# Modulation of a hybrid diffusion backbone: conditioning rows by DMA, sums of squares on VectorE, other pacing of the modulation sums

## The chip, the cores and the metric

The kernel runs on 1 core of one Trainium2 chip. Its engines are TensorE (PE in the profile; PEld is its loading of weights), VectorE (DVE), ScalarE (ACT), GpSimd (POOL) and SyncE (SP), which here only issues transfers. The metric is the device time of one execution in microseconds, the median of several.

## The reference

The reference is a backbone of two layers over 512 latent tokens and 256 context tokens, 1024 channels wide, batch 1, all in float32. Cut to what matters here:

```python
for l in range(2):
    mod_l = split(silu(c) @ w_mod[l] + b_mod[l], 6)        # latent: shift, scale, gate, twice
    mod_c = split(silu(c_ctx) @ w_mod[l] + b_mod[l], 6)    # context
    h  = rms_norm(x, norm1_g[l]) * (1 + mod_l[1]) + mod_l[0]
    hc = rms_norm(xc, norm1_g[l]) * (1 + mod_c[1]) + mod_c[0]
    # one input projection of h and hc, three mixers (neighbourhood attention, gated
    # recurrence, windowed attention), a branch projection each, merged by sigmoid gates: m
    x = x + mod_l[2] * (m @ w_out[l])
    h2 = rms_norm(x, norm2_g[l]) * (1 + mod_l[4]) + mod_l[3]
    x = x + mod_l[5] * (square(relu(h2 @ w_ff1[l])) @ w_ff2[l])
    # in layer 0 the context xc goes through the same with mod_c; layer 1 only reads it
return rms_norm(x, final_g)
```

In layer 1 the context needs only its first shift and scale, since it is not updated there. The modulation has 48 chunks of 128 output channels in each layer (8 chunks for each of the 6 parts).

## The kernel before

Channels lie on the 128 partitions and tokens on the free axis: a tensor of 1024 channels is 8 tiles of 512 latent and 256 context columns. Each float32 product is made of three passes over rounded high and low parts (`PASSES`, L310), so each weight tile is loaded by SP (L248), rounded by ScalarE (L258) and subtracted on DVE (L259), four tiles ahead of its use.

The program is written in one order by hand, and that order is each instruction's priority; a planner then sets each engine's own order, and an instruction can be put ahead of its place in the program when what it needs is there. Each engine then runs its list in order. All large tiles of SBUF come from one pool of 50 slots (`t3`).

Work beside the main chain of products is written as generators. `pump` (L183) is called after each group of matmuls with the time that they should take; each side queue (`attn`, `lru`, `misc`) takes one step of its generator whenever a `period` of such time has come together. `finish_but(side, n)` steps a queue at once until n generators are left.

`sil_rows` (L387) makes the silu of both conditioning vectors as rows on all partitions: 16 broadcast products with the identity on PE (L394), evacuated by ScalarE (L395). `mod_chunks` (L402) is the modulation: w_mod lies transposed in memory, so for each chunk of output channels and each half of the 1024 inputs a tile of 128 x 512 is loaded (L411), and for each of latent and context one instruction of DVE (L420) multiplies it with the row and sums along the free axis. After 16 tiles the sums of 8 chunks are closed (L430 to L437): `gt1` is the gate of the first residual, `G1` and `G2` are the scales of the two norms. Chunks 0 to 15 of layer 0 are made otherwise, at the start. In layer 0, chunks 16 to 23 (the first gate), 24 to 39 (shift and scale of the second norm) and 40 to 47 (the last gate) are put into `misc` when the gates and the last branch begin (L1196 to L1200), with two tiles loaded ahead; all of layer 1 follows during the MLP of layer 0 (L1297 to L1300), with six.

The output projection (L1233 to L1255) makes column tiles 0 to 3 for both segments, then 4 to 7 for the latent columns, then 4 to 7 for the context. `x_add` (L1231) adds each to the residual stream, and `Sumsq.add` (L474, L479) squares the result on ScalarE and adds the squares up: the first 6 of 7 adds on POOL, the last on DVE. `rstd` sums over partitions by PE (L484), takes the power -0.5 on POOL (L487) with one Newton step on DVE, and spreads the result by PE (L495). `n2` makes the normed and modulated tiles (`normed`, L508 to L510). The MLP starts with `gemm_first` (L337). After layer 1, `n1` writes the output of the final norm (L1331, L1334), in two halves of 256 columns.

Of the kernel before, what the change touches and what calls it, by code (L numbers as in the profile page):

```python
# [9 lines left out]
AF = mybir.ActivationFunctionType  # L10
ALU = mybir.AluOpType
# [3 lines left out]
D = 1024  # L15
# [3 lines left out]
L = 2  # L19
P = 128  # L20
# [5 lines left out]
NFF = 8  # L26
WA = 4
LB = 3.436
PM1 = 1.954
MA = 2  # L30
PS = 0.75
RK = 1
POOLSS = 8
NF = 1
NG = 1
BA = ((1, 1, 1, 1), (2, 2, 0, 0))
# [10 lines left out]
WH = 12  # L47
PA = 1.789
PL = 1.398
PM = 1.106  # L50
HPS = {'gate10': 60, 'ws': -50, 'relu': 60, 'gate01': 60, 'xp': 60, 'gx': 20, 'sink1': 400}
GO = [(x[0], int(x[1]), int(x[2])) for x in GO]
EPS = 1e-6
# [65 lines left out]
def build(tc, A, out):  # L119
    nc = tc.nc  # L120

    with ExitStack() as es:
# [11 lines left out]
        def t3(name, dt=F32):  # L134
            cnt[0] += 1
            return big.tile([P, W], dt, tag="t3", name=f"{name}_{cnt[0]}")
# [24 lines left out]
        def ps_s():  # L161
            cnt[0] += 1
            return pss.tile([P, 512], F32, tag="S", name=f"S_{cnt[0]}")
# [124 lines left out]
        class Seg:  # L288
            def __init__(self, s, cols, ps):
                self.s, self.cols, self.ps = s, cols, ps  # L290
                self.n = cols.stop - cols.start
# [77 lines left out]
        mk = [const.tile([P, 2, 2], F32, name=f"mk{k}") for k in range(8)]  # L369
        xsp = drp.tile([8, P, T], F32, name="xsp")  # L370

        nc.scalar.dma_start(cc, A["cc"])
        nc.sync.dma_start(kc[:, 0:K_PERM], A["kc"][:, 0:K_PERM])
        for l in range(L):
            nc.scalar.dma_start(sm[l], A["sm"][l])
# [10 lines left out]

        def sil_rows():  # L387

            for n in range(4):
                silB.append(t3("sil"))  # L390
                ps = ps_s()
                for k in range(4):
                    c = 2 * (4 * (n % 2) + k) + n // 2
                    mm(ps[:, k * P:(k + 1) * P], sil[:, c:c + 1].to_broadcast([P, P]), ident, start=True, stop=True)  # L394
                act(silB[n][:, 0:512], ps, AF.Copy)  # L395
            silB.append(t3("junk"))

        def finish_but(side, n):
            while len(side.q) > n:
# [2 lines left out]
        def mod_chunks(l, lo, hi, ahead):  # L402

            seq = [(c, i) for c in range(lo, hi) for i in range(2)]
            raws = deque()

            def ld(n):
                if n < len(seq):
                    c, i = seq[n]
                    r = t3("mr")  # L410
                    nc.sync.dma_start(r[:, 0:512], A["w_mod"][l, c][:, i * 512:(i + 1) * 512])  # L411
                    raws.append(r)

            for n in range(ahead):
                ld(n)
            yield
            for n, (c, i) in enumerate(seq):
                r = raws.popleft()
                for s in range(2):
                    V.scalar_tensor_tensor(  # L420
                        r[:, 0:512] if s else silB[4][:, 0:512], r[:, 0:512], 1.0, silB[2 * s + i][:, 0:512], op0=ALU.mult, op1=ALU.mult, accum_out=mpart[:, i, s, c:c + 1]
                    )
                    yield
                r = None
                ld(n + ahead)
                if n % 16 == 15:
                    g = c // 8
                    cs = slice(8 * g, 8 * g + 8)
                    for s in range(2):
                        V.tensor_tensor(modT[l][:, s, cs], mpart[:, 0, s, cs], mpart[:, 1, s, cs], op=ALU.add)  # L430
                        V.tensor_tensor(modT[l][:, s, cs], modT[l][:, s, cs], sm[l][:, O_BM + 8 * g:O_BM + 8 * g + 8], op=ALU.add)
                        if g == 1:
                            V.scalar_tensor_tensor(G1[l][:, s], modT[l][:, s, cs], 1.0, sm[l][:, O_N1:O_N1 + 8], op0=ALU.add, op1=ALU.mult)
                        if g == 2:
                            V.tensor_scalar(gt1[l][:, s], modT[l][:, s, cs], 0.5, None, op0=ALU.mult)
                        if g == 4:
                            V.scalar_tensor_tensor(G2[l][:, s], modT[l][:, s, cs], 1.0, sm[l][:, O_N2:O_N2 + 8], op0=ALU.add, op1=ALU.mult)  # L437
# [23 lines left out]


        class Sumsq:
            def __init__(self, pool=POOLSS):
                self.pool = pool
                self.acc = {}
                self.n = {}

            def add(self, x, seg):
                s = t3("sq")  # L470
                c = seg.cols
                a = self.acc.get(seg)
                with hp("ss"):
                    act(s[:, c], x[:, c], AF.Square)  # L474
                    if a is None:
                        self.acc[seg] = s
                    else:
                        self.n[seg] = self.n.get(seg, 1) + 1
                        (nc.gpsimd if self.n[seg] < self.pool else V).tensor_tensor(a[:, c], a[:, c], s[:, c], op=ALU.add)  # L479

        def rstd_sum(acc, seg, ps):
            nt = seg.n // P
# [170 lines left out]
            x.append(t)  # L653
        x0 = x
        hs0 = hs = []
        ss0 = ss = Sumsq(0)
        for k in range(8):
            ss.add(x[k], SL)
        rbl = t3("rb")
# [85 lines left out]
        for l in range(L):  # L745
# [448 lines left out]
                    gate(("wi", l, 34 + j), gb[-1])  # L1194
            finish(lru)
            if l == 0:  # L1196
                sil_rows()
                misc.period = PM
                for lo, hi in ((16, 24), (24, 40), (40, 48)):
                    misc.add(mod_chunks(0, lo, hi, MA))  # L1200
            mhl = []
# [13 lines left out]
                branch(yb, 1, jp, sink2)  # L1215
            yb = h = m = None
            finish_but(misc, 2)


            wide[0] = 1 if WIDE & 2 else 0  # L1220
# [56 lines left out]
            for fb in range(NFF + 1):  # L1277
                if fb < NFF:
                    lst = [pair("a") for _ in range(4)]
                    af[fb] = lst  # L1280
                    if fb == 0:
                        rs_ = [t3("r") for _ in range(4)]

                        def mlp_done(i, seg, ps):
                            with hp("relu"):
                                relu2(rs_[i], ps, seg)
                            if seg is HS[0] and i < 3:
                                return
                            for n in range(4) if seg is HS[0] else (i,):
                                relu2_end(rs_[n], lst[n], seg.cols)  # L1290

                        got = [w_get("w1", l, i) for i in range(4)]
                        w_ahead()
                        gemm_first(got.__getitem__, h2, HS, mlp_done, range(4), [(range(4), range(8))])
                        got = None
                        rs_ = None
                        if l + 1 < L:  # L1297
                            finish(misc)
                            misc.period = PM1
                            misc.add(mod_chunks(l + 1, 0, 48, 6))  # L1300
                    else:
                        for i in range(4):
                            w = w_get("w1", l, 4 * fb + i)
                            w_ahead()
                            r = t3("r")
                            for seg in FS:
                                relu2(r, gemm1(w, 0, h2, seg), seg)
                            relu2_end(r, lst[i], CA)
                if fb > 0:
                    if fb == NFF:  # L1310
                        wide[0] = 1 if WIDE & 8 else 0
                    a = af.pop(fb - 1)
# [6 lines left out]
                    if fb == NFF:  # L1319
                        order = [(jp, seg, (0, 1)) for seg in HS for jp in range(4)]  # L1320
                        hs = []

                        def n1(seg, k, rb, x=x, hs=hs, l=l):
                            if l + 1 < L:
                                normed(hs, k, x[k], rb, G1[l + 1][:, seg.s, k:k + 1], modT[l + 1][:, seg.s, k:k + 1], seg, seg.s == 0)
                                return
                            if k % 2 == 0:
                                fin.append(t3("out"))
                            o = fin[-1]
                            i = k % 2  # L1330
                            V.scalar_tensor_tensor(o[:, i * 256:(i + 1) * 256], x[k][:, seg.cols], sm[0][:, O_FG + k:O_FG + k + 1], rb, op0=ALU.mult, op1=ALU.mult)  # L1331
                            if i:
                                q0 = seg.cols.start - PAD
                                nc.sync.dma_start(out[k - 1:k + 1, :, q0:q0 + 256].rearrange("k p n -> p k n"), o[:, 0:512].rearrange("p (k n) -> p k n", k=2))  # L1334

                        fin = []

                        def second(ss=ss, n1=n1, seg=HS[1]):
                            rb = rstd(ss.acc[seg], seg)
                            for k in range(8):  # L1340
                                n1(seg, k, rb)

                    for jp, seg, jjs in order:
# [22 lines left out]
def layouts(np, i):  # L1366
# [16 lines left out]
    xt = np.concatenate([i["x"][0], i["ctx"][0]], axis=0)  # L1383
    d["xc"] = np.ascontiguousarray(xt.T).reshape(8, P, T)
    cc = np.stack([i["c"][0], i["c_ctx"]], axis=0)
    d["cc"] = np.ascontiguousarray(cc.reshape(2, 8, P).transpose(2, 1, 0)).reshape(P, 16)
    d["w_mod"] = np.ascontiguousarray(i["w_mod"].transpose(0, 2, 1)).reshape(L, 48, P, D)
    d["w_mod0"] = np.ascontiguousarray(i["w_mod"][0, :, 0:2048].reshape(8, P, 2, 8, P).transpose(3, 1, 0, 2, 4)).reshape(8, P, 2048)
    d["w_in"] = cols(i["w_in"], 1024)
# [84 lines left out]
```

## Time and profile before

| | |
|---|---|
| time, median of 3 runs (lowest to highest) | 2294.87 us (2293.21 to 2295.03) |
| the profiled execution's own time | 2291.37 us |
| its span, first to last instruction | 2289.6 us |
| PE busy | 2258.2 us, 99% |
| DVE busy | 1477.4 us, 65% |
| ACT busy | 1016.4 us, 44% |
| POOL busy | 93.6 us, 4% |
| mean granted TensorE clock | 0.994 |

The span is one execution. Matmuls are pipelined, so the length of one overlaps the next: where a busy PE has no gaps, the distance of two starts is what one costs. The granted clock is a share of full speed, 2.4 GHz; the lower level is 1.2 GHz. Idle time of an engine other than the one that sets the pace costs nothing.

### The profile page before, as it was taken

What the parts mean: (1) busy time and instruction counts of PE and PEld (TensorE: products, weight loads), DVE (VectorE), ACT (ScalarE), POOL (GpSimd) and SP (SyncE); (2) the same over time, 40 slices, a digit from 0 to 9 for tenths busy, and PEclk for the clock granted to TensorE, in tenths of its full rate; (3) what the DMA queues carried; (4) which work ended last, traced back from release to release, by engine and by line L of the source; (5) the groups of instructions that cost most, each with busy time, mean ns of one, the idle gap of its engine ahead of it and who ended that gap; (6) DMA issues with size and microseconds to landing.
All of it is one profiled execution on the core that took longest, in us unless ns stands there. A gap on an engine that the chain in (4) does not pass through costs nothing.

```text
span 2289.6 us, 34042 instructions
## 1 busy us (share of the span) xinstructions
PE 2258.2 (99%) x13364; PEld 1918.0 (84%) x13364; DVE 1477.4 (65%) x3149; ACT 1016.4 (44%) x1868; POOL 93.6 (4%) x78
## 2 busy tenths in 40 slices
PE   8999999999999999999999999999999999999998
PEld 6888888888888888888888887888888789888887
DVE  5776545677668998776665468664467776444444
ACT  4666545667622242222222246654575844332331
POOL 0000000000100200000000020000000102000001
PEclk8999999999999999999999999999999999999999
DMA  7101111112135343343332132112112242222221
GB/s 275 65 32 44 47 65 50 34 51 70 65 124 199 133 170 129 134 138 129 103 120 95 65 118 77 56 47 74 52 60 88 88 148 93 101 92 100 93 92 65
DMA packets 79856, 216.58 MB, mean 95 GB/s; under 512 B 9296, under 2 KB 12496, under 8 KB 79696
## 3 DMA queue, kind: packets, MB, share of 16 engines
q1 hardware_dynamic: 79264, 214.27, 27.0%
q8 instruction: 105, 1.72, 0.3%
q14 instruction: 55, 0.45, 0.1%
q10 hardware_dynamic: 432, 0.14, 0.0%
HBM read 208.08 MB, written 5.24 MB: 93 GB/s over the span
## 4 chain that ended last, share of the span: by engine, by line
PE 88%; DVE 7%; ACT 3%; issue 1%; DMA 1%; POOL 0%; ACTq 0%; POOLq 0%; DVEq 0%; SPq 0%
PE gl L310 38%; PE S L310 30%; PE gc L310 5%; PE O L616 4%; PE S L598 3%; PE gl L337 2%; PE S L546 2%; PE S L547 2%; DVE wl L259 1%; PE S L337 1%; DVE mr L420 1%; DVE junk L420 1%; ACT tau L1071 1%; DMA wm<-in_w_mod_dram 1%; ACT wh L258 0%
## 5 line engine op out<-in xcount | busy, mean ns | idle before, releaser
L259 DVE TENSOR_TENSOR wl<-wr,wh 128x1024 fp32r<-128x1024 f32 (+1 forms) x276 | 333.8, 1210 | 281.5 <-PE S L310 101.9
L258 ACT ACTIVATE wh<-wr 128x1024 fp32r<-128x1024 f32 (+1 forms) x276 | 287.9, 1045 | 444.2 <-DMA wr<-in_w_ff_dram 254.3
L310 PE MATMUL gl<-hh,wh 128*128 128x512 f32 (+1 forms) x936 | 353.3, 377 | 4.7 <-DVE KL L789 2.1
L310 PE MATMUL gl<-hh,wl 128*128 128x512 f32 (+1 forms) x936 | 347.9, 372 | 0.0
L310 PE MATMUL gl<-hl,wh 128*128 128x512 f32 (+1 forms) x936 | 347.0, 371 | 0.0
L310 PE MATMUL S<-hh,wl 128*128 128x512 f32 (+1 forms) x704 | 247.8, 352 | 1.0 <-DVE wl L259 1.0
L310 PE MATMUL S<-hh,wh 128*128 128x512 f32 (+1 forms) x704 | 247.8, 352 | 0.2 <-ACT tau L1071 0.2
L310 PE MATMUL S<-hl,wh 128*128 128x512 f32 (+1 forms) x704 | 246.9, 351 | 0.0
L310 PEld LDWEIGHTS gl<-hh,wh 128*128 128x128 f32 x936 | 176.1, 188 | 37.7 <-issue 10.1
L310 PEld LDWEIGHTS gl<-hl,wh 128*128 128x128 f32 x936 | 176.3, 188 | 32.6 <-issue 0.9
L310 PEld LDWEIGHTS gl<-hh,wl 128*128 128x128 f32 x936 | 176.2, 188 | 25.6 <-issue 0.5
L310 PEld LDWEIGHTS S<-hh,wh 128*128 128x128 f32 x704 | 132.3, 188 | 20.4 <-ACT tau L1071 0.4
L310 PEld LDWEIGHTS S<-hh,wl 128*128 128x128 f32 x704 | 132.2, 188 | 20.4 <-DVE wl L259 1.5
L310 PEld LDWEIGHTS S<-hl,wh 128*128 128x128 f32 x704 | 132.4, 188 | 19.9 <-issue 0.3
L574 ACT ACTIVATE P<-S,s 128x512 f32<-128x512 f32 (+1 forms) x160 | 102.9, 646 | 84.6 <-DVE s L570 41.2
L310 PE MATMUL S<-ah,wl 128*128 128x512 f32 (+1 forms) x384 | 137.0, 357 | 0.0
L310 PE MATMUL S<-al,wh 128*128 128x512 f32 (+1 forms) x384 | 136.8, 356 | 0.0
L310 PE MATMUL S<-ah,wh 128*128 128x512 f32 (+1 forms) x384 | 136.6, 356 | 0.0
L420 DVE SCALAR_TENSOR_TENSOR junk<-mr,sil 128x512 f32<-128x512 f32 x160 | 110.6, 691 | 24.2 <-DMA mr<-in_w_mod_dram 24.1
L310 PE MATMUL gl<-ah,wl 128*128 128x512 f32 (+1 forms) x352 | 124.3, 353 | 0.0
L310 PE MATMUL gl<-al,wh 128*128 128x512 f32 (+1 forms) x352 | 124.3, 353 | 0.0
L310 PE MATMUL gl<-ah,wh 128*128 128x512 f32 (+1 forms) x352 | 124.2, 353 | 0.0
(344 smaller groups left out, 4836.7 us busy)
## 6 DMA issues: line engine op xcount, KB each, us to landing
wr<-in_w_ff_dram SPq DMA_DIRECT2D x128, 512.0 KB, 3.5
wr<-in_w_in_dram SPq DMA_DIRECT2D x100, 512.0 KB, 3.5
mr<-in_w_mod_dram SPq DMA_DIRECT2D x160, 256.0 KB, 4.4
wr<-in_w_branch_dram SPq DMA_DIRECT2D x24, 512.0 KB, 3.5
wm<-in_w_mod_dram SPq DMA_DIRECT2D x32, 256.0 KB, 6.0
wr<-in_w_out_dram SPq DMA_DIRECT2D x16, 512.0 KB, 3.6
bias<-in_bias_dram SPq DMA_DIRECT2D x16, 256.0 KB, 4.0
x<-in_xc_dram SPq DMA_DIRECT2D x8, 384.0 KB, 7.1
```

Source lines behind the costliest of these rows:

```text
L258: act(h_, r, AF.Copy)
L259: V.tensor_tensor(l_, r, f(h_), op=ALU.subtract)
L310: mm(o, w[wi_][:, c0 + k * P:c0 + (k + 1) * P], view(acts[k][xi]), start=(k == 0 and i == 0), stop=(k == n - 1 and i == 2))
L337: mm(os_[i], w[wi_][:, k * P:(k + 1) * P], seg.nat(acts[k][xi]), start=(k == 0 and p_ == 0), stop=(k == n - 1 and p_ == 2))
L420: V.scalar_tensor_tensor(r[:, 0:512] if s else silB[4][:, 0:512], r[:, 0:512], 1.0, silB[2 * s + i][:, 0:512], op0=ALU.mult, op1=ALU.mult, ...
L546: mm(d, qs[:, qc:qc + P], rk, start=True, stop=False)
L547: mm(d, qs[:, qc:qc + P], rl, start=False, stop=True)
L574: act(p[:, 0:n0], self.S[i][:, 0:n0], AF.Exp, bias=nm[:, i:i + 1], accum_out=su[:, i:i + 1])
L598: nc.tensor.transpose(d, self.p[i][:, j * P:(j + 1) * P], ident)
L616: mm(o[half, oc:oc + P], vt[:, vc:vc + 64], h["pt"][:, j * P:(j + 1) * P], start=(j == 0), stop=(j == nt - 1), tile_position=(0, 64 * h["h ...
L1071: act(tau[ax][half, seg.cols], z[HALF[ax]], AF.Tanh, scale=0.5, bias=bcol)
```

## The change

The two conditioning vectors come a second time in the input `cc`, along the free axis and repeated on all 128 partitions, and `sil_rows`, now a generator at the head of `misc`, loads them and makes the silu with a Tanh on ScalarE and one instruction on DVE each; its factor 0.5 goes into L420. `Sumsq.add` does all adds on DVE. In layer 1 the sums of the context are left out from chunk 16 on. The pacing has other periods: `PM` 1.25 instead of 1.106, a new one of 2.4 (`PMW`) from the output projection of layer 0 on, and `PM1` 2.35 instead of 1.954; the last chunks of layer 0 are finished one block of the MLP later. In the last half of the output two of eight tiles are made by ScalarE and POOL and written by ScalarE's queue.

```diff
-PM1 = 1.954
+PM1 = 2.35
-POOLSS = 8
-PM = 1.106
+PM = 1.25
+PMW = 2.4
...
-        nc.scalar.dma_start(cc, A["cc"])
+        nc.scalar.dma_start(cc, A["cc"][:, 0:16])
...
         def sil_rows():
 
+            for n in range(5):
+                silB.append(t3("sil"))
+                if n < 4:
+                    nc.sync.dma_start(silB[n][:, 0:512], A["cc"][:, 16 + 512 * n:16 + 512 * (n + 1)])
+            yield
             for n in range(4):
-                silB.append(t3("sil"))
-                ps = ps_s()
-                for k in range(4):
-                    c = 2 * (4 * (n % 2) + k) + n // 2
-                    mm(ps[:, k * P:(k + 1) * P], sil[:, c:c + 1].to_broadcast([P, P]), ident, start=True, stop=True)
-                act(silB[n][:, 0:512], ps, AF.Copy)
-            silB.append(t3("junk"))
+                act(silB[4][:, 0:512], silB[n][:, 0:512], AF.Tanh, scale=0.5)
+                V.scalar_tensor_tensor(silB[n][:, 0:512], silB[4][:, 0:512], 1.0, silB[n][:, 0:512], op0=ALU.add, op1=ALU.mult)
+                yield
...
+            ns = lambda c: 2 if l + 1 < L or c < 16 else 1
...
-                for s in range(2):
+                for s in range(ns(c)):
                     V.scalar_tensor_tensor(
-                        r[:, 0:512] if s else silB[4][:, 0:512], r[:, 0:512], 1.0, silB[2 * s + i][:, 0:512], op0=ALU.mult, op1=ALU.mult, accum_out=mpart[:, i, s, c:c + 1]
+                        r[:, 0:512] if s else silB[4][:, 0:512], r[:, 0:512], 0.5, silB[2 * s + i][:, 0:512], op0=ALU.mult, op1=ALU.mult, accum_out=mpart[:, i, s, c:c + 1]
                     )
...
-                    for s in range(2):
+                    for s in range(ns(c)):
                         V.tensor_tensor(modT[l][:, s, cs], mpart[:, 0, s, cs], mpart[:, 1, s, cs], op=ALU.add)
...
             def add(self, x, seg):
...
-                with hp("ss"):
-                    act(s[:, c], x[:, c], AF.Square)
-                    if a is None:
-                        self.acc[seg] = s
-                    else:
-                        self.n[seg] = self.n.get(seg, 1) + 1
-                        (nc.gpsimd if self.n[seg] < self.pool else V).tensor_tensor(a[:, c], a[:, c], s[:, c], op=ALU.add)
+                act(s[:, c], x[:, c], AF.Square)
+                if a is None:
+                    self.acc[seg] = s
+                else:
+                    V.tensor_tensor(a[:, c], a[:, c], s[:, c], op=ALU.add)
...
             if l == 0:
-                sil_rows()
                 misc.period = PM
+                misc.add(sil_rows())
                 for lo, hi in ((16, 24), (24, 40), (40, 48)):
                     misc.add(mod_chunks(0, lo, hi, MA))
...
             finish_but(misc, 2)
+            misc.period = PMW
...
                         if l + 1 < L:
-                            finish(misc)
                             misc.period = PM1
                             misc.add(mod_chunks(l + 1, 0, 48, 6))
...
                 if fb > 0:
+                    if fb == 1 and l + 1 < L:
+                        finish_but(misc, 1)
...
-                        def second(ss=ss, n1=n1, seg=HS[1]):
+                        def second(ss=ss, n1=n1, seg=HS[1], x=x, l=l):
                             rb = rstd(ss.acc[seg], seg)
-                            for k in range(8):
+                            if l + 1 == L:
+
+                                xg = t3("xg")
+                                for i in range(2):
+                                    act(xg[:, i * 256:(i + 1) * 256], x[6 + i][:, seg.cols], AF.Copy, scale=sm[0][:, O_FG + 6 + i:O_FG + 7 + i])
+                                rbs = t3("rb")
+                                act(rbs[:, 0:256], rb, AF.Copy)
+                                for i in range(2):
+                                    nc.gpsimd.tensor_tensor(xg[:, i * 256:(i + 1) * 256], xg[:, i * 256:(i + 1) * 256], rbs[:, 0:256], op=ALU.mult)
+                                nc.scalar.dma_start(out[6:8, :, 256:512].rearrange("k p n -> p k n"), xg[:, 0:512].rearrange("p (k n) -> p k n", k=2))
+                            for k in range(8 if l + 1 < L else 6):
                                 n1(seg, k, rb)
```

## Rows read from the trace of the kernel before

**Rows 1.** The page: busy us of each engine, share of the span, instructions.
```profile
PE 2258.2 (99%) x13364; PEld 1918.0 (84%) x13364; DVE 1477.4 (65%) x3149; ACT 1016.4 (44%) x1868; POOL 93.6 (4%) x78
```
**Rows 2.** Stretches of 50 us: busy us of each engine, clock, DMA share.
```profile
750.00:800.00 50.00, 46.41 (x257) 40.55 (x256) 45.95 (x114) 10.13 (x15) 11.68 (x9) 0.97 0.31 106
...
850.00:900.00 50.00, 50.00 (x287) 43.60 (x286) 49.66 (x120) 14.67 (x22) 0.00 (x0) 1.00 0.45 153
...
1300.00:1350.00 50.00, 49.12 (x282) 42.41 (x282) 24.52 (x40) 13.11 (x22) 11.36 (x9) 1.00 0.31 106
```
**Rows 3.** What PE waited for, whole span: us in total, times, longest.
```profile
PE S L484 <- DVE sq L479: 5.1, 2, 3.6
```
**Rows 4.** PE's timeline: start, us of one, instruction, idle before it and releaser.
```profile
785.16 0.28 PE L310 MATMUL gl<-mmh,wh 128*128 128x256 f32 x1
...
787.64 0.28 PE L310 MATMUL gl<-mmh,wh 128*128 128x256 f32 x1
791.52 1.35 PE L484 MATMUL S<-ones,sq 128*128 128x1 f32 x8 [3.59 <-DVE sq L479]
...
793.09 0.41 PE L310 MATMUL gl<-mml,wh 128*128 128x256 f32 x1
...
795.60 0.28 PE L310 MATMUL gl<-mml,wh 128*128 128x256 f32 x1
...
803.73 0.40 PE L337 MATMUL gl<-hh,wh 128*128 128x512 f32 x1
```
**Rows 5.** Two stretches of the output projection: PE, PEld, DVE, ACT, POOL, clock.
```profile
743.40:787.30 43.90, 43.90 (x235) 37.51 (x235) 43.57 (x107) 8.97 (x13) 12.92 (x9) 1.00 0.48 168
...
791.50:795.50 4.00, 3.98 (x21) 3.98 (x22) 2.33 (x6) 0.42 (x1) 1.04 (x1) 0.58 0.23 68
```
**Rows 6.** The tile of the conditioning rows: ns least, median, most; first and last start.
```profile
L394 PE MATMUL S<-kc,sil x32: 270/275/275, 658.5 to 661.9; 128*128 128x128 f32 x32
```
**Rows 7.** DVE's timeline in the output projection of layer 0.
```profile
753.81 1.26 DVE L431 TENSOR_TENSOR modT<-modT,sm 128x8 f32<-128x8 f32 x1
...
781.68 0.69 DVE L420 SCALAR_TENSOR_TENSOR mr<-mr,sil 128x512 f32<-128x512 f32 x1
...
787.04 0.28 DVE L437 SCALAR_TENSOR_TENSOR G<-modT,sm 128x8 f32<-128x8 f32 x2
...
789.26 0.74 DVE L1231 SCALAR_TENSOR_TENSOR x<-S,gt,x 128x512 f32<-128x512 f32 x1
...
797.90 0.75 DVE L508 SCALAR_TENSOR_TENSOR nt<-x,G,S 128x512 f32<-128x512 f32 x1 [0.99 <-PE S L495]
799.50 0.75 DVE L510 SCALAR_TENSOR_TENSOR hl<-nt,modT,hh 128x512 fp32r<-128x512 f32 x1 [0.85 <-ACT hh L509]
```
**Rows 8.** POOL's timeline: an add of 512 columns, and one of 256.
```profile
753.41 1.64 POOL L479 TENSOR_TENSOR sq<-sq,sq 128x512 f32<-128x512 f32 x1 [3.99 <-ACT sq L474]
...
2278.24 0.72 POOL L479 TENSOR_TENSOR sq<-sq,sq 128x256 f32<-128x256 f32 x1 [0.69 <-ACT sq L474]
```
**Rows 9.** The tile of the squares, adds on DVE: ns least, median, most.
```profile
L479 DVE TENSOR_TENSOR sq<-sq,sq x22: 417/426/695, 6.0 to 2279.6; 128x256 f32<-128x256 f32 x13, 128x512 f32<-128x512 f32 x9
```
**Rows 10.** Stretches of L420 on DVE alone: busy us (events, two per sum), clock.
```profile
662.20:703.30 41.10, 21.40 (x64) 1.00 0.45 149
...
852.00:902.00 50.00, 27.09 (x81) 1.00 0.46 156
```
**Rows 11.** The chain that ended last: start, us, what.
```profile
687.41 5.57 PE gl L310 x24
```
**Rows 12.** SP's timeline: transfers issued.
```profile
766.70 4.01 SPq L411 DMA_DIRECT2D mr<-in_w_mod_dram  x8
```
**Rows 13.** Timelines of PE and of DVE at the end.
```profile
2282.31 0.71 PE L495 MATMUL S<-kc,r 128*128 128x128 f32 x4 [1.62 <-DVE r L490]
...
2283.06 3.22 DVE L1331 SCALAR_TENSOR_TENSOR out<-x,sm,S 128x256 f32<-128x256 f32 x8 [0.81 <-PE S L495]
```
**Rows 14.** Groups by shape: a copy of 256 columns from PSUM, busy us, mean ns.
```profile
L601 ACT ACTIVATE P<-S 128x256 f32<-128x256 f32 x32 | 11.3, 382 | 8.8 <-PE S L598 8.8
```

More of the change, by code (lines that the diff above doesn't have):

```diff
@@ L463, in build, with __init__ @@
         class Sumsq:
-            def __init__(self, pool=POOLSS):
-                self.pool = pool
+            def __init__(self):
                 self.acc = {}
-                self.n = {}
             def add(self, x, seg):
@@ L655, in build @@
         hs0 = hs = []
-        ss0 = ss = Sumsq(0)
+        ss0 = ss = Sumsq()
         for k in range(8):
@@ L1385, in layouts @@
     cc = np.stack([i["c"][0], i["c_ctx"]], axis=0)
-    d["cc"] = np.ascontiguousarray(cc.reshape(2, 8, P).transpose(2, 1, 0)).reshape(P, 16)
+    d["cc"] = np.concatenate([cc.reshape(2, 8, P).transpose(2, 1, 0).reshape(P, 16), np.broadcast_to(cc.reshape(1, 2 * D), (P, 2 * D))], axis=1)
     d["w_mod"] = np.ascontiguousarray(i["w_mod"].transpose(0, 2, 1)).reshape(L, 48, P, D)
```

## The prediction

> **What bounds the kernel now.** I read the busy shares first. TensorE (PE) is busy for 2258.2 of 2289.6 us [rows 1], so only two things can move the time: matmuls that go away, and PE's 31 us of idle time. The table by 50 us stretches says where that idle time lies. From 850 to 1300 us there is none, even where VectorE (DVE) is busy for 49.66 of 50 us; 3.6 us lie between 750 and 800, 0.9 between 1300 and 1350 [rows 2]. Of the waits of PE the longest is that of L484, the sum of squares over partitions, for the add of L479: 5.1 us in two places [rows 3]. The larger place is in layer 0, in the second half of the output projection: PE stops at 787.8 and goes on at 791.52, and then issues a 256-column matmul every 0.21 us (0.41 shown) until 795.60, where 0.28 is shown and one starts every 0.12 [rows 4]. The table gives the reason: granted clock 0.58 from 791.5 to 795.5, between the two levels of 1.2 and 2.4 GHz, behind an idle PE [rows 5]. So the stop cost 3.6 us of idle time and 4.0 x 0.42 = 1.7 us of clock, 5.3 us in all.
>
> Why was the add late? From 743.4 to 787.3 DVE was busy for 43.57 of 43.9 us, and GpSimd (POOL) ran nine adds of L479, 12.92 us [rows 5]. The DVE timeline has the x_add of the last column tile at 789.26, some 4 us after PE went on to the next tile at 785.16, behind modulation sums of L420 and small operations [rows 4, 7]. DVE lost time to POOL as well: an L431 over eight elements took 1.26 us and ended at 755.07, as the POOL add did that began at 753.41 [rows 7, 8]. Nine DVE instructions of that stretch are lengthened in this way, by 0.42 to 1.1 us, 7.6 us together.
>
> **The conditioning rows.** Removed are 16 broadcast products; the trace has 32 PE instructions for them, 658.4 to 661.9 us, 275 ns each and one every 0.11 us [rows 6]. PE works without a break on both sides, so this is 3.5 us off its path. In their place come four loads of 256 KB on SP, some 0.5 us of issue each by the eight like them [rows 12], ahead of the weight loads of that moment; weights are split four tiles ahead, so 2 us of delay is covered; without that cover it would be up to 2 us. Four Tanh replace four Copies of the same size on ScalarE (the gates around them are Tanh too), and four scalar_tensor_tensor of 0.69 us are new on DVE: 2.8 us, hidden, since PE does not wait there. The load of cc still moves 64 bytes for each partition, now with a stride: nothing, and at most some tenths at the start.
>
> **The pacing.** A step is one generator step, one L420 mostly. The pump counts 5.12 units for 24 matmuls of 512 columns, which take 5.57 us [rows 11]: 1.09 us per unit. From the start of the modulation to the output projection there are 4 gates x 7.68 + 8 branch halves x 3.84 = 61.4 units. Before: 61.4 / 1.106 = 55 steps; the first chunk takes 34 (one to load, 32 sums, one to close), 37.6 units or 41 us, and the trace has its 32 sums between 662.2 and 703.3 [rows 10]: the count holds. 21 steps go into the second chunk, the 64 sums behind shift and G2 of the second norm. After: 49 steps, of which 6 are the conditioning rows and 34 the first chunk, leaving 9. Up to the forced finish in the last third of the output projection there are 4 x 7.68 + 4 x 5.12 + 2.56 = 53.8 units: 48 steps before, which ends the chunk, and 53.8 / 2.4 = 22 after. So 30 sums stand ahead of the forced finish and 34 in a lump behind it, in front of the first n2 on DVE.
>
> Whether that lump hurts depends on whether DVE runs sums ahead of their place in the program. In layer 1's chunks it does: in 852 to 902 us there are 81 events, two per sum, so 40 sums, where the pace of 1.954 units (2.13 us) sets 23 [rows 10]. Loads do too: eight were issued from 766.70 on [rows 12], six tiles beyond the pace. I take it that free DVE time is filled this way. Then DVE's work from 743.4 to G2 decides. G2 was done at 787.3 [rows 7]. Added: by the pace 13 sums of the second chunk are done at 743.4 where 22 were, so 9 more at 0.69 us [rows 7], 6.2 us (bounds: 0 if DVE runs ahead as in layer 1, 9.7 if only 8 are done). Added: nine adds on DVE, six at 0.69 and three at 0.42 [rows 9], 5.4 us. Gone: the 7.6 us that POOL took (bounds 0 and 12.9). That gives 791.3. Needed is G2 at: first w1 matmul at 803.73 less the 5.3 us of the stop, 798.4, less the 2.35 us from the L508 at 797.90 to the end of its L510 [rows 4, 7]: 796.0. So the lump is in time with 5 us to spare, and the x_add, which now stands ahead of it, is taken at once: the 5.3 us of the stop go.
>
> One rule speaks against this. The Trainium skill, "Perfetto Trace Analysis", section "Optimizing Scalar/DVE Operations", advises moving work off a saturated DVE, GpSimd included, though it adds that the two share an SBUF port and this may not help; the change moves adds onto a saturated DVE. By the advice alone G2 would be at 787.3 + 6.2 + 5.4 = 798.9, 2.9 us late, and the total about -3.
>
> By the rows, POOL's adds held DVE for 7.6 us, more than the 5.4 that they cost there; I keep 791.3.
>
> In layer 1 DVE is spared 64 sums, 44 us, between 840 and 1225, where PE never idles [rows 2]: nothing. Moving the last chunk's finish past the next w1 block likewise.
>
> **The other adds.** At the end of layer 0 DVE sets the pace for some 10 us within 1300 to 1350 (PE idle 0.88) [rows 2]; six adds of 0.42 fall in there, less what POOL held: +0.7 (bounds 0 and +2). In the output projection of layer 1 I take nothing (bounds -1 and +1).
>
> **The tail.** The eight L1331 of the last half take 3.22 us from 2283.06, 0.40 each; two go to ScalarE and POOL: -0.8 for DVE. The other way starts at the same rb (2283.02) [rows 13]: a copy from PSUM of 0.38 [rows 14], two multiplies of some 0.72 [rows 8], and its DMA at about 2285.0, before DVE's last at 2285.5. So -0.8 (bounds 0 and -1.2).
>
> **Sum.** -3.5 -5.3 +0.7 -0.8 = -8.9 us. The profiled execution took 2291.37 (span 2289.6), so 2282.5; the median of the runs shown is 2294.87, 3.5 above, so I forecast 2286.0.
>
> **The rivals.** (1) The lump is late, by place: DVE fills little ahead, since tiles or loads are short. Sums stay where the program puts them: 34 x 0.69 = 23.5 us from about 789, G2 at 812.5, first w1 matmul at 814.9 instead of 798.4: 16.5 us idle and some 2 us at the lower clock, so -8.9 + 18.5 = +9.6: 2304. It decides once G2 is later than 796 by more than 9 us. For it: the trace before never ran the second chunk ahead. Against it: sums and loads that ran ahead [rows 10, 12]. (2) G2 slips by a few us, because DVE fills its gaps only partly, or POOL's 7.6 us do not come back (798.9 instead of 791.3): 3 to 6 us idle with the clock behind it, in total about -3: 2292. For it: DVE's 43.57 of 43.9 us; against it: that the lengthened rows end with POOL's adds [rows 5, 7, 8]. The advice cited above would end here. (3) The stop stays, since DVE's order still puts sums before the last x_add: only matmuls and tail go, -3.6: 2291. For it: in 743 to 787 DVE had no gap; against it: POOL's part of that goes.
>
> **How the numbers follow.** Forecast 0.48, rival 1 0.17, rival 2 0.20, rival 3 0.15. The measurement can tell about 0.2% (4.6 us) from no change. Faster by more: 0.45 of the forecast's 0.48 and 0.07 of rivals 2 and 3, 0.52. Slower: rival 1 and a bad end of 2, 0.18. Within: 0.30. The range goes from 2281 (all lower bounds, -12, and the spread of the runs) to 2300, which leaves out the full form of rival 1; the likeliest case by itself has 2281 to 2290.
>
> **What would show it.** Right: no matmul at the line of the broadcast; the wait of L484 in layer 0 under 1 us and clock 1.00 there; no L431 over 1 us; G2 before 796 less 3.5; the last out write 0.8 us sooner against the last matmul. Wrong: PE idle in front of the first w1 matmuls of layer 0, with L508 waiting for the L437 of G2; or PE idle in a new place.

## The result and the profile after

The changed kernel takes 2311.2 us (median of 4 runs, 2310.71 to 2312.92) where the kernel before takes 2294.69: a ratio of 1.0075, interval 1.0057 to 1.0092, 16.5 us slower. The profiled execution took 2310.88 us, with a span of 2309.1. Several line numbers are shifted: the sums of L420 are L423 now, their loads L414, the add of squares L478, the sum over partitions L483, the spread L494, the first instruction of `n2` L507, the last tiles L1332.

I first read the busy shares on the page of the changed kernel, which answer to [rows 1], and the stretches that answer to [rows 2, 5], with the columns of those.

```profile
PE 2256.9 (98%) x13332; PEld 1915.6 (83%) x13332; DVE 1456.4 (63%) x3061; ACT 1019.0 (44%) x1871; POOL 43.6 (2%) x32
```

```profile
750.00:800.00 50.00, 45.15 (x263) 39.19 (x261) 31.84 (x77) 9.11 (x13) 1.04 (x1) 0.99 0.40 133
800.00:850.00 50.00, 30.52 (x151) 25.48 (x152) 44.09 (x116) 15.20 (x27) 0.70 (x1) 0.77 0.25 86
...
743.40:787.30 43.90, 43.90 (x236) 37.35 (x234) 28.74 (x69) 8.62 (x12) 1.04 (x1) 1.00 0.24 81
```

DVE now has room where it had none: 28.74 of 43.9 us before 787.3, against 43.57 [rows 5]. But right behind, PE works for only 30.52 of 50 us. The waits of PE say for what, and its timeline shows where:

```profile
PE gl L337 <- ACT hh L508: 25.0, 2, 23.5
...
PE S L483 <- DVE sq L478: 1.8, 1, 1.8
```

```profile
783.73 1.05 PE L483 MATMUL S<-ones,sq 128*128 128x1 f32 x8
...
788.04 1.16 PE L494 MATMUL S<-kc,r 128*128 128x128 f32 x8 [0.67 <-DVE r L489]
...
819.28 0.80 PE L337 MATMUL gl<-hh,wh 128*128 128x512 f32 x1 [23.46 <-ACT hh L508]
819.87 0.63 PE L337 MATMUL gl<-hh,wl 128*128 128x512 f32 x1
820.30 0.63 PE L337 MATMUL gl<-hl,wh 128*128 128x512 f32 x1
```

The stop of [rows 4] is gone: L483 begins with no wait; the 1.8 us left are those of the tail. In its place PE waits 23.46 us for the first normed tile, and then starts a matmul of 512 columns every 0.43 us where the first experiment below has 0.23. DVE's timeline has the reason: the first half of the second chunk (the sums of chunks 24 to 31, for the shift) closes at 779.57, the other half stands behind the square root (L485), and G2 (L440) behind that.

```profile
779.57 0.29 DVE L434 TENSOR_TENSOR modT<-modT,sm 128x8 f32<-128x8 f32 x2
781.54 0.75 DVE L1231 SCALAR_TENSOR_TENSOR x<-S,gt,x 128x512 f32<-128x512 f32 x1 [1.68 <-PE S L310]
...
784.82 0.16 DVE L485 TENSOR_SCALAR v<-S 128x4 f32<-128x4 f32 x1 [1.14 <-PE S L483]
...
790.02 0.69 DVE L423 SCALAR_TENSOR_TENSOR sil<-mr,sil 128x512 f32<-128x512 f32 x1 [1.20 <-DMA mr<-in_w_mod_dram]
...
816.51 0.69 DVE L423 SCALAR_TENSOR_TENSOR mr<-mr,sil 128x512 f32<-128x512 f32 x1
...
817.53 0.28 DVE L440 SCALAR_TENSOR_TENSOR G<-modT,sm 128x8 f32<-128x8 f32 x2
817.73 0.74 DVE L507 SCALAR_TENSOR_TENSOR nt<-x,G,S 128x512 f32<-128x512 f32 x1
```

The view of stretches for L423 alone (two events per sum) counts them: 22 sums from 730 to 784.8, and 32 from there to G2. The next fence has the stretches of all engines again, where the clock stands beside PE's idle time:

```profile
730.00:784.80 54.80, 14.90 (x44) 1.00 0.38 139
784.90:817.60 32.70, 21.11 (x64) 0.71 0.63 217
```

```profile
799.00:819.00 20.00, 0.00 (x0) 0.00 (x0) 19.13 (x58) 2.60 (x3) 0.00 (x0) 0.50 0.43 159
819.30:823.00 3.70, 3.70 (x10) 2.87 (x11) 2.91 (x5) 1.12 (x3) 0.00 (x0) 0.57 0.00 0
823.00:827.00 4.00, 4.00 (x19) 3.22 (x18) 3.51 (x8) 1.66 (x3) 0.00 (x0) 1.00 0.45 131
```

With PE idle the granted clock is 0.50, the lower level; it is 0.57 for 3.7 us after the start, 1.6 us of work lost. SP's timeline, against [rows 12], shows the loads of those sums:

```profile
759.62 2.33 SPq L414 DMA_DIRECT2D mr<-in_w_mod_dram  x5
785.52 0.33 SPq L248 DMA_DIRECT2D wr<-in_w_ff_dram  x1
785.94 2.76 SPq L414 DMA_DIRECT2D mr<-in_w_mod_dram  x6
792.06 0.33 SPq L248 DMA_DIRECT2D wr<-in_w_ff_dram  x1
792.49 6.60 SPq L414 DMA_DIRECT2D mr<-in_w_mod_dram  x10
```

Before, between the same two weight loads, it had

```profile
766.32 0.33 SPq L248 DMA_DIRECT2D wr<-in_w_ff_dram  x1
766.70 4.01 SPq L411 DMA_DIRECT2D mr<-in_w_mod_dram  x8
793.53 7.52 SPq L248 DMA_DIRECT2D wr<-in_w_ff_dram  x2
```

so eight loads from 766.70 on; now five at 759.62, then none until a weight load that waited 23.5 us for PE to free its tile went out at 785.52.

The account by stretches, from events that both traces have (the matmul that waits for L868/L867 `Q`, DVE's first instruction on `gb`, L1150/L1149, the last matmul of the output projection, the spread at the end of layer 0, the last matmul of w2):

| stretch | before | after | difference |
|---|---|---|---|
| start to `Q` | 90.86 | 90.57 | -0.3 |
| to the first `gb` (conditioning rows) | 574.19 | 570.93 | -3.3 |
| to the end of the output projection | 138.68 | 134.32 | -4.4 |
| PE idle in front of w1 | 0 | 23.46 | +23.5 |
| first w1 matmul to the end of layer 0 | 534.59 | 536.71 | +2.1 |
| layer 1, to the last w2 matmul | 939.93 | 940.75 | +0.8 |
| to the end | 11.35 | 12.36 | +1.0 |

The sum is +19.4, the spans differ by 19.5. The medians differ by 16.5 only: the profiled execution of before was 3.3 us faster than its median here, that of after 0.3. In which stretch those 3 us lie the table can't say.

### The profile page after: what moved, and what is told of

Same layout as the page of the kernel before. It is cut to its first block, busy times and chain, and to the rows that moved or that the text cites. A ratio compares the mean times of both kernels' runs of the same rounds, so it can differ in the third digit from the quotient of the medians.

```text
span 2309.1 us, 33849 instructions
## 1 busy us (share of the span) xinstructions
PE 2256.9 (98%) x13332; PEld 1915.6 (83%) x13332; DVE 1456.4 (63%) x3061; ACT 1019.0 (44%) x1871; POOL 43.6 (2%) x32
## 4 chain that ended last, share of the span: by engine, by line
PE 90%; DVE 5%; ACT 2%; issue 2%; DMA 1%; POOL 0%; SPq 0%; DVEq 0%; POOLq 0%; ACTq 0%
PE gl L310 38%; PE S L310 31%; PE gc L310 5%; PE O L615 4%; PE S L597 3%; PE gl L337 2%; PE S L545 2%; PE S L546 2%; PE S L337 1%; DVE wl L259 1%; DMA wr<-in_w_in_dram 1%; ACT tau L1070 1%; DVE KL L788 0%; DVE mr L423 0%; DVE sil L423 0%
## 5 line engine op out<-in xcount | busy, mean ns | idle before, releaser
L423 DVE SCALAR_TENSOR_TENSOR sil<-mr,sil 128x512 f32<-128x512 f32 x160 | 109.9, 687 | 33.4 <-DMA mr<-in_w_mod_dram 32.7
```

The costliest lines, as they stand in the source:

```text
L423: V.scalar_tensor_tensor(r[:, 0:512] if s else silB[4][:, 0:512], r[:, 0:512], 0.5, silB[2 * s + i][:, 0:512], op0=ALU.mult, op1=ALU.mult, ...
```

## The experiments

The theory (T): the lump of sums behind `finish_but(misc, 1)` costs all of the loss, and the rest of the change gains about what was forecast. The first rival (R1): the adds moved to DVE made it late. Ratios are to the kernel before on the same chip.

**The old pace, all else as changed.**

```diff
-PM = 1.25
-PMW = 2.4
+PM = 1.106
+PMW = 1.106
```

> The kernel after, with both periods of the modulation in layer 0 back at 1.106 (PM and PMW); conditioning rows, adds on VectorE and the new tail stay. Theory T (the lump): the slower pace leaves 32 sums of the second chunk, and their loads, in one lump ahead of the first tile of the second norm, and TensorE waits 23.5 us for it. With the old pace the lump is 2 or 3 sums, G2 is done before 796 us, the first w1 matmul waits under 2 us, and of the forecast's -8.9 us all is left but the tail's error of 1.8: about 2287.6 us (2284 to 2291). Rival R1 (the adds): VectorE is late because it has taken over the nine adds of GpSimd, 5.4 us of work in the stretch before G2; the pace only says where the sums stand. Then G2 stays late, the wait of the first w1 matmul stays over 10 us, and the time is 2300 to 2311.

Measured: 2286.91 us, 0.9970 (0.9959 to 0.9981). Two sums are left behind the square root, G2 starts at 788.86, PE waits for nothing in front of w1. Its first two w1 matmuls:

```profile
794.57 0.39 PE L337 MATMUL gl<-hh,wh 128*128 128x512 f32 x1
794.80 0.40 PE L337 MATMUL gl<-hh,wl 128*128 128x512 f32 x1
```

R1 has fallen: the adds are still on DVE.

**The new pace alone, in the kernel before.**

```diff
-PM = 1.106
+PM = 1.25
+PMW = 2.4
...
             finish_but(misc, 2)
+            misc.period = PMW
```

> The kernel before, with the two periods of layer 0 alone (1.25 for the gates and branches, 2.4 from the output projection on). Everything else is that of before, the broadcast products and the adds on GpSimd too. Theory T: 26 to 30 sums stand in the lump; at 0.73 us each, with two weight subtractions of 1.22 between, from about 790 us on, G2 comes at 811 to 815 instead of 787, and TensorE waits some 10 to 15 us in front of w1, with about 2 us of clock behind it, while the stop of 5.3 us at the sum over partitions goes, since fewer sums stand ahead of the last x_add: 2303 to 2309 us. Rival R1 (the adds) expects no change: 2293 to 2296.

Measured: 2308.8 us, 1.0066 (1.0051 to 1.0081): 26 sums in the lump, and 18.95 us of wait in front of w1 (here L338):

```profile
818.11 0.80 PE L338 MATMUL gl<-hh,wh 128*128 128x512 f32 x1 [18.95 <-ACT hh L510]
```

The wait is above the 10 to 15 expected: with the stop gone PE was ready at 799.16, where before began w1 at 803.73, and G2 came at 816.36, later than 811 to 815. The wait of the sum over partitions in layer 0 is gone here with the adds still on GpSimd.

**GpSimd's adds back in the changed kernel.**

```diff
-                    V.tensor_tensor(a[:, c], a[:, c], s[:, c], op=ALU.add)
+                    (nc.gpsimd if self.n[seg] < 8 else V).tensor_tensor(a[:, c], a[:, c], s[:, c], op=ALU.add)
```

> The kernel after, with the adds of the squares back on GpSimd (the first six of seven); pace, rows and tail as after. Theory T: the lump is the same 32 sums, so the wait in front of w1 stays at 20 us or more, and the time is that of after within 3 us: 2308 to 2314. Rival R1 (the adds on VectorE made it late): G2 is earlier by some 5 us and more, the wait shrinks by as much, 2290 to 2305.

Measured: 2310.23 us, 1.0074 (1.0059 to 1.0089), again 32 sums in the lump and a wait of 23.2 us.

**The loads earlier, at the new pace.** Each sum keeps its place in the program; only the second chunk's loads are issued 18 tiles ahead, in a second run 10.

```diff
-                    misc.add(mod_chunks(0, lo, hi, MA))
+                    misc.add(mod_chunks(0, lo, hi, 18 if lo == 24 else MA))
```

> The kernel after, with 18 instead of 2 tiles of the second chunk loaded ahead of their sums; the pace, and so the place of each sum in the program, stays. Two forms of theory T differ here. T1 (the loads): a sum can go ahead of its place in the program, but its load can't, since it stands two tiles ahead of it, behind weight loads on SP that wait for TensorE; with the loads early VectorE runs the sums in its gaps of 729 to 790 us (some 15 us of them, and the 22 us after), the lump is gone, and the time is 2285 to 2291. T2 (the place): the sums stay where the pace puts them whatever is loaded, the wait stays at 15 us or more: 2303 to 2311. If the gaps suffice for half of the sums only, 2295 to 2300.

> The kernel after, with 10 instead of 2 tiles of the second chunk loaded ahead of their sums (the fourth experiment had 18). If a sum goes ahead of its place exactly as far as its load does, eight tiles more ahead take 16 of the 32 sums out of the lump; at the changed kernel's 0.73 us a sum, with its weight subtractions, that is 11.7 us of the 23.5: the wait in front of w1 is 10 to 13 us and the time 2298 to 2301. If instead the lump depends on room that appears all at once (the fourth experiment had none left), the time lies at one of the two ends, 2287 or 2311.

Measured with 18: 2287.42 us, 0.9970 (0.9960 to 0.9980). With 10: 2300.84 us, 1.0029 (1.0018 to 1.0039), a wait of 11.89 us in front of w1. The stretches of L423 alone and the first w1 matmul, first of the kernel with 18, then of that with 10:

```profile
730.00:784.80 54.80, 31.66 (x94) 1.00 0.42 151
784.90:789.20 4.30, 0.00 (x0) 1.00 0.39 122
...
795.71 0.39 PE L337 MATMUL gl<-hh,wh 128*128 128x512 f32 x1
```

```profile
730.00:785.60 55.60, 22.89 (x68) 1.00 0.37 134
785.70:806.90 21.20, 10.63 (x32) 0.85 0.68 236
...
808.53 0.79 PE L337 MATMUL gl<-hh,wh 128*128 128x512 f32 x1 [11.89 <-ACT hh L508]
```

With 2, 10 and 18 tiles ahead there are 32, 16 and 0 sums behind the square root, two fewer for each tile more, and waits of 23.46, 11.89 and 0 us. So DVE does take sums ahead of their place, as far as their loads are early. The form T2 (the place of the sum alone) has fallen.

**The loads on another queue.** The load stays two tiles ahead and goes out by ScalarE's queue, in a second run by GpSimd's.

```diff
-                    nc.sync.dma_start(r[:, 0:512], A["w_mod"][l, c][:, i * 512:(i + 1) * 512])
+                    (nc.scalar if lo == 24 else nc.sync).dma_start(r[:, 0:512], A["w_mod"][l, c][:, i * 512:(i + 1) * 512])
```

> The kernel after, with the loads of the second chunk's tiles issued by ScalarE's queue instead of SP's; still two tiles ahead, same pace. It tells apart why the loads of the lump come late. Form Q (the queue): they are held on SP behind a weight load that waits 23.5 us for TensorE to free a weight tile; on ScalarE's queue they go at once, VectorE fills its gaps, 2286 to 2292. Form S (two ahead of the sum, in a slot that is free only then): the load of a sum in the lump asks for a tile that a square or another sum of the last column tiles still holds, whatever queue it is on; the lump stays, the wait in front of w1 is 18 us or more: 2304 to 2312.

> The kernel after, with the loads of the second chunk's tiles issued by GpSimd's queue, where next to nothing else stands; still two tiles ahead, same pace. On ScalarE's queue the loads stood between squares that wait for x_add, so that run did not free them of every other wait; this one does. Form Q (the queue: held behind a weight load): the lump goes, 2286 to 2292. Form S (the load's own place, two tiles ahead of its sum): the lump stays at 32 sums, the wait at 18 us or more, 2304 to 2314.

Measured: 2314.6 us (1.0091, 1.0073 to 1.0110) and 2316.74 us (1.0098, 1.0080 to 1.0117), two executions each, both somewhat above the range of form S; the lump is 32 sums in both, the wait in front of w1 25.26 and 26.48 us. GpSimd's timeline in the second:

```profile
743.19 0.55 POOL L414 DMA_DIRECT2D mr<-in_w_mod_dram  x1 [12.06 <-DVE sq L478]
786.22 1.04 POOL L486 TENSOR_TENSOR r<-v,nhalf 128x4 f32<-128x4 f32 x1 [42.48 <-DVE v L485]
787.23 4.32 POOL L414 DMA_DIRECT2D mr<-in_w_mod_dram  x8
```

So the weight load on SP is not needed for the lump: on ScalarE's queue the loads stand between squares that wait for x_add, and on the nearly empty queue of GpSimd behind the power of the square root, which waits 42.48 us for DVE. A general shortage of slots in SBUF is unlikely too, since with 18 ahead sixteen tiles more had room. What in the planner holds a load to its place more than a sum stays open; these runs show only that it does, on three queues.

**The parts alone, in the kernel before.** First the adds, then the conditioning rows (made at once, where the products stood).

```diff
-                        (nc.gpsimd if self.n[seg] < self.pool else V).tensor_tensor(a[:, c], a[:, c], s[:, c], op=ALU.add)
+                    V.tensor_tensor(a[:, c], a[:, c], s[:, c], op=ALU.add)
```

> The kernel before, with all adds of the squares on VectorE; pace, broadcast products and tail of before. The prediction's step: the stop of 5.3 us in the output projection of layer 0 goes, and 0.7 are paid at the end of layer 0, so -4.6: about 2289.5 us. Rival: with the old pace VectorE was busy for 43.57 of 43.9 us there, the nine adds of 5.4 us more make the last add of that stretch and G2 late, the stop stays or moves to the first w1 matmul, 3 to 6 us: 2294 to 2298. A second rival, now that the slow pace has cleared the stretch of sums in the changed kernel: it was the pace that took the stop away, and the adds do nothing either way: 2293 to 2295.

Measured: 2287.67 us, 0.9973 (0.9962 to 0.9983), 1.8 us less than the step gives; the output projection's stretch is 5.2 us shorter. DVE's groups of lines in the output projection, in the kernel before (743 to 788 us) and here (741 to 786):

```profile
L420 DVE SCALAR_TENSOR_TENSOR mr<-mr,sil 128x512 f32<-128x512 f32 x21 | 17.5, 835 | 0.3
L420 DVE SCALAR_TENSOR_TENSOR junk<-mr,sil 128x512 f32<-128x512 f32 x22 | 16.1, 731 | 0.0
L259 DVE TENSOR_TENSOR wl<-wr,wh 128x1024 fp32r<-128x1024 f32 x3 | 4.7, 1577 | 0.0
...
L431 DVE TENSOR_TENSOR modT<-modT,sm 128x8 f32<-128x8 f32 x4 | 2.8, 710 | 0.0
```

```profile
L420 DVE SCALAR_TENSOR_TENSOR junk<-mr,sil 128x512 f32<-128x512 f32 x23 | 15.8, 686 | 0.0
L420 DVE SCALAR_TENSOR_TENSOR mr<-mr,sil 128x512 f32<-128x512 f32 x22 | 15.0, 684 | 0.1
L475 DVE TENSOR_TENSOR sq<-sq,sq 128x512 f32<-128x512 f32 (+1 forms) x10 | 6.1, 606 | 0.0
L259 DVE TENSOR_TENSOR wl<-wr,wh 128x1024 fp32r<-128x1024 f32 x4 | 4.9, 1219 | 0.0
...
L431 DVE TENSOR_TENSOR modT<-modT,sm 128x8 f32<-128x8 f32 x4 | 0.7, 163 | 0.0
```

The same instructions take 835, 731, 1577 and 710 ns on average beside GpSimd's adds, and 684, 686, 1219 and 163 without: with the counts of before that is 7.4 us. DVE does ten adds (L475, 6.1 us) more in the stretch, and G2 is not later for it: it is done at 784.63 instead of 787.32, where 2.35 us of the difference are a shorter start of this execution, up to `Q`. The stop is gone, as the sum over partitions (L480 here) shows:

```profile
785.57 0.95 PE L480 MATMUL S<-ones,sq 128*128 128x1 f32 x8
```

```diff
-                act(silB[n][:, 0:512], ps, AF.Copy)
+                act(silB[4][:, 0:512], silB[n][:, 0:512], AF.Tanh, scale=0.5)
+                V.scalar_tensor_tensor(silB[n][:, 0:512], silB[4][:, 0:512], 1.0, silB[n][:, 0:512], op0=ALU.add, op1=ALU.mult)
```

> The kernel before, with the conditioning rows alone loaded along the free axis (Tanh and one VectorE instruction each, made at once where the broadcast products stood); pace, adds and tail of before. The prediction's step: 32 matmul instructions, 3.5 us, leave TensorE's unbroken work: 2290.6 us (2289.5 to 2291.5). Rival: everything from there on comes 3.5 us sooner against VectorE's work, which is full up to the stop, so the stop grows by what was gained: 2293 to 2295.

Measured: 2289.74 us, 0.9982 (0.9973 to 0.9991), 4.6 us faster, within the range of the step. The stretches show both the step and its rival: that from `Q` to `gb` is 3.2 us shorter, and the stop grows from 3.59 to 4.88 us, since DVE's work does not come sooner. So the rows explain less than 3.2 of the 4.6 us, and the agreement with the step is in part luck. The start of this execution, to `Q`, is 2.7 us shorter than that of before; starts differ by that much between kernels with the same instructions up to there (last section). What the rest of the 4.6 us is stays open.

**The tail.** The first experiment without the new tail, and the kernel before with only the parts of layer 1 and the tail:

```diff
-                            for k in range(8 if l + 1 < L else 6):
+                            for k in range(8):
```

> The first experiment (changed kernel, both periods at 1.106) without the new tail: all eight last tiles on VectorE, as before. The prediction's step had the new tail at -0.8 us; the trace of the changed kernel has 12.36 us from the last w2 matmul to the end where before has 11.35, because VectorE's first instruction waits for ScalarE's copy of the row. If that reading holds, this kernel is 1.0 us faster than the first experiment: about 2285.9 us; if the step holds, 0.8 slower: 2287.7. Either is inside what a median can tell by itself, so the stretch from the last w2 matmul to the end decides: 11.4 us against 12.4.

```diff
-PM1 = 1.954
+PM1 = 2.35
...
-                for s in range(2):
+                for s in range(ns(c)):
...
-                            for k in range(8):
+                            for k in range(8 if l + 1 < L else 6):
```

> The kernel before, with what the change does later than the first norm of the MLP alone: layer 1's sums of the context left out from chunk 16 on, its period at 2.35, the last chunk of layer 0 finished one w1 block later, and two of the last eight tiles made by ScalarE and GpSimd. Pace in layer 0, adds and broadcast products stay. The prediction's steps: nothing in layer 1, -0.8 us in the tail: 2294.1 less 0.8, 2293.3. By the trace of the third experiment, which has GpSimd's adds and the new tail, 12.10 us from the last w2 matmul to the end against 11.35: +0.7, 2294.9. A gain of over 2 us would show that the sums of layer 1 cost something after all.

Measured: 2287.0 us, 0.9969 (0.9957 to 0.9981), the same as with the new tail, and 2294.84 us, 1.0005 (0.9996 to 1.0014), no change. From the last w2 matmul to the end: 11.34 to 11.35 us in three kernels with GpSimd's adds and the old tail, 12.10 (the third experiment) and 11.63 (the kernel before with the parts of layer 1 and the tail) with GpSimd's adds and the new tail, 11.99 and 12.47 with DVE's adds and the old one, 12.13 to 12.74 with both new. My reading that the new tail is the whole cost has fallen. Some of it is the clock: the last spread takes 0.71 us in the kernel before [rows 13] and 1.22 in the changed one, at a granted clock of 0.50, which is 0.5 of its 1.0:

```profile
2301.07 1.22 PE L494 MATMUL S<-kc,r 128*128 128x128 f32 x4 [1.68 <-DVE r L489]
```

Without the last spread the stretch is 10.6 us with GpSimd's adds and the old tail, 10.9 with the new tail alone, 11.2 and 11.3 with DVE's adds alone, 11.1 to 11.5 with both. So the new tail alone costs 0.3 us, the adds alone 0.6 to 0.7, both 0.5 to 0.9, and what the last spread costs comes and goes between kernels. In the kernel before with the parts of layer 1 and the tail, DVE's first output waits for ScalarE's copy of the row; first DVE's timeline, then ScalarE's:

```profile
2286.30 2.44 DVE L1333 SCALAR_TENSOR_TENSOR out<-x,sm,S 128x256 f32<-128x256 f32 x6 [1.22 <-ACT rb L1348]
```

```profile
2285.88 0.38 ACT L1348 ACTIVATE rb<-S 128x256 f32<-128x256 f32 x1 [2.76 <-PE S L496]
```

**A pick of what paid.** Rows, adds on DVE except in the last layer's MLP, the old pace, the old tail.

```diff
-PM = 1.25
-PMW = 2.4
+PM = 1.106
+PMW = 1.106
...
-            ss = Sumsq()
+            ss = Sumsq(8 if l else 0)
```

> A pick of what paid: conditioning rows by load, adds on VectorE but for those of the last layer's MLP, which stay on GpSimd, both periods at 1.106, the old tail. From the traces: rows -3.2, the stop -5 with some of it given back at the next w1 block, and the last stretch at 11.34 us as in the three kernels that had adds on GpSimd there, against 12.0 to 12.7 in those that had not: about 2286 us (2284.5 to 2287.5), some 1 us below the first experiment. If the longer tail was chance, it is the first experiment's 2287.

Measured: 2285.87 us, 0.9962 (0.9948 to 0.9976): faster than both kernels, but not told apart from the first experiment. The last stretch took 11.81 us, not 11.34: its last spread ran 1.22 us, 0.5 over that of before. The parts don't add up in the medians: rows alone gave 4.6 us and adds alone 6.7, both together 8.3 here and 7.2 in the first experiment. In that one's stretches the rows (-3.2) and the output projection (-4.8) are there in full, and layer 1 is 3.3 us longer than before; how much of that is the edit and how much the execution is not shown.

## Why the prediction was wrong

The forecast was 2286.0; the changed kernel takes 2311.2, beyond the range. Rival 1 came true, and larger than it was priced.

- **The step that failed**: "I take it that free DVE time is filled this way." Free time came, and was not filled. The pump arithmetic held (30 sums ahead and 34 in the lump forecast, 32 counted), the added and freed DVE work held as well, but the 32 sums never went into the free time, because their loads did not. The rows that I read as "runs ahead" were of another setting: [rows 10] is layer 1, with six tiles loaded ahead, and the loads of [rows 12] stood between two weight loads in SP's list, where (so I read it now) the old pace had put them. With two tiles ahead a slower pace moves the loads back with the sums. Loaded 18 ahead, the same program came to 2287.42.
- **The size of rival 1**: 16.5 us of idle time forecast, 23.46 measured. The lump took 27.1 us from 790.02 (32 sums, and three weight subtractions of 1.22, three x_adds and a wait of 1.48 that I had left out), so w1 began at 819.28 instead of 814.9; and PE was ready at 795.8 instead of 798.4: the prediction's sum took the stop off that point, but not the rows' gain, which only its signs name. So G2 was needed earlier than the 796.0 that it worked out. The clock behind it cost 1.6 us, 2 forecast.
- **Rows**, -3.5: right, -3.3 in its stretch; but alone part of it went into a longer stop. In the first experiment some went into a wait of 1.25 us behind the first w1 block, where ScalarE's relu (L1271) stands behind a weight's rounding.
- **The stop**, -5.3: right, -4.4 in its stretch, and -5.2 with the adds alone. The cause is shown twice: it goes with GpSimd's adds (the adds alone, pace unchanged), and it goes with the sums that the slow pace takes out of the stretch (the second experiment). So the slow pace had nothing left to gain.
- **GpSimd's hold on DVE**, 7.6 us taken back against 5.4 added: right, 7.4 by the means above. The advice cited from the Trainium skill ("Perfetto Trace Analysis", section "Optimizing Scalar/DVE Operations") would have been wrong here, as moving the adds onto DVE alone gave 0.9973. Its own caveat, that the two share an SBUF read port, agrees with the 835 against 684 ns; that it is the port no run shows.
- **The other adds**, +0.7 at the end of layer 0: not seen. With the adds alone the stretch from w1 to there is 533.80 us against 534.59; after, it is 2.1 us longer, of which the clock has 1.6.
- **Layer 1 and the late finish**, nothing: not told from nothing, 1.0005 with the new tail in it. **The tail**, -0.8: wrong in sign, +1.0, of which 0.5 is the clock in the last spread and some the adds on DVE. The prediction let both ways start at the same rb. In the kernel before with the new tail, DVE starts behind ScalarE's copy, 0.42 us later, and that kernel takes 4.0 us from DVE's last tile to its end, where before took 3.3.

## What to carry to other kernels

A paced side stream has two places for each step: that of the work and that of its load. Before taking a full engine's free time as a gain, look at which loads have been issued by then: here two sums more went ahead for each tile more that was loaded ahead, and with two tiles ahead next to none did. And price a lump in front of a critical instruction with all that stands in the same engine's list, weight subtractions too.

## What was not expected of the hardware

The start differs from execution to execution: the matmul that waits for `Q` began between 88.15 and 91.65 us in the fourteen kernels, whose instructions are the same up to there but for the layout of `cc`, so single spans differ by as much as some of the terms that were forecast; only short stretches between common events made those readable. A long one is no better than a span: layer 1 up to the last w2 matmul took 939.34, 939.93 and 941.95 us in three kernels (the second experiment, before, the rows alone) that have the same layer 1. A load of a modulation tile issued by GpSimd took it 0.54 us, one by SP 0.33 to 0.38.
